# Moving the matmul operands of a two-layer hybrid-attention kernel to other byte places in SBUF

## The chip, the cores and the metric

The kernel runs on one core of a Trainium2 chip. The metric is the device time of one execution in microseconds (us). Before the change three runs took 823.54, 824.45 and 826.3 us; the median is 824.45 us.

## What is computed

Two transformer layers on 256 tokens of width 1024, all in float32. Each layer modulates its input by six vectors made from `silu(c) @ w_ada`, projects it, runs a top-k sparse attention and a latent attention, merges them by gates, and ends in a convolutional feed-forward block. Both halves close with a layer norm over a residual. Cut to what matters here:

```python
for l in range(DEPTH):                                   # DEPTH = 2
    mod = jax.nn.silu(c) @ w_ada[l] + b_ada[l]
    sh1, sc1, g1, sh2, sc2, g2 = jnp.split(mod[:, None, :], 6, axis=-1)
    h = x * (1.0 + sc1) + sh1
    y = token_mixer(h, ...)                              # h @ w_in, dsa and mla attention, gates, w_out
    x = layer_norm(DEEPNORM_ALPHA * x + g1 * y, ln1_g[l], ln1_b[l])
    h = x * (1.0 + sc2) + sh2
    y = conv_ffn(h, w_up[l], conv_w[l], conv_b[l], w_down[l])
    x = layer_norm(DEEPNORM_ALPHA * x + g2 * y, ln2_g[l], ln2_b[l])
```

## The kernel before

All weights lie in one stream in HBM. `load` (line 206) fetches them in pieces of up to 1 MB into four `raw` buffers through SyncE's queue. TensorE is to multiply in one pass per product, on four-byte operands of reduced precision (`float32r`), so each weight piece of 1024 columns is split: ScalarE copies its rounded part into a tile `hi` (line 241), VectorE subtracts that from the raw piece into a tile `lo` (line 242). There are four buffers of each. The activations are split in the same way into pairs: `hh` and `hl` for the input of a projection (lines 422 and 423), `nh` and `nl` for the normed inputs of the latent attention, `ybh`/`ybl` and `yah`/`yal` for the attention outputs, and six pairs `h2h`/`h2l` for the hidden layer of the feed-forward block.

`mm3` (line 284) is the heart of the kernel: three matmuls per product, `hi` by `hh`, `hi` by `hl` and `lo` by `hh`. The weight half, 128 columns of 4 bytes in each partition, is the operand that is loaded into the array; the activation half, 256 columns, is streamed through it. In the profile every such matmul is one LDWEIGHTS (row PEld) and one MATMUL (row PE), both of line 286. The load for a matmul goes on while the matmul ahead of it is streaming. In the value projection (line 606) the roles are exchanged: `hh`/`hl` are loaded and `hi`/`lo` are streamed. In line 592, 512 columns of `hi`/`lo` are streamed against `nh`/`nl`. Logits, transposes, sums and three pieces of `w_ada` (line 258) are plain float32 matmuls.

The order within a layer: `g1` (first projections), `qa` and `va` with the scoring, `uq`/`uk`/`uv` with the top-k search, the gates `ga`/`gb` woven with the two attentions, the branches `wb`/`wa`, `wo` with the layer norm, `up` and eighteen `upp` groups of 48 matmuls, `dn` with the second layer norm. A scheduler sets the order of the instructions on each engine, and gives each tile its place.

Places are given out pool by pool: first the pool `cp` of lasting tiles, then `wp` of streamed weights and scratch, then `ap_` of activations. In a pool each tag has its buffers in the order in which tags were first used, each rounded up to 32 bytes; every partition has the same places. The lines in question:

```python
cp = ctx.enter_context(tc.tile_pool(name="cp", bufs=1))                                  # 141
wp = ctx.enter_context(tc.tile_pool(name="wp", bufs=1))                                  # 142
ap_ = ctx.enter_context(tc.tile_pool(name="ap", bufs=1))                                 # 143
...
t = wp.tile([P, 2048], F32, name=f"raw{u}", tag="raw", bufs=RAW)                         # 206
...
hi = wp.tile([P, 1024], F32R, name=f"hi{i}", tag="whi", bufs=NHI)                        # 235
lo = wp.tile([P, 1024], F32R, name=f"lo{i}", tag="wlo", bufs=NLO)                        # 236
...
for p in passes:                                                                         # 285
    PE.matmul(out, whl[p // 2][:, wcol], xhl[p % 2][xsl], start=start and p == 0, stop=stop and p == 2,
              skip_group_check=True)
...
hh[0] = ap_.tile([P, KD, T], F32R, name=f"hh{name}", tag="hh")                           # 422
hh[1] = ap_.tile([P, KD, T], F32R, name=f"hl{name}", tag="hl")                           # 423
...
iw8 = ap_.tile([P, 2, HEADS], F32, name=new("iw8"), tag="iw8")                           # 484
```

Slices of a weight half start at multiples of 512 bytes in its tile, slices of an activation half at multiples of 1024 bytes, so modulo 256 bytes every slice has the place of its tile.

Of the kernel before, what the change touches and what calls it, by code (L numbers as in the profile page):

```python
# [9 lines left out]
F32 = mybir.dt.float32  # L10
# [7 lines left out]
P = 128  # L18
# [4 lines left out]
HEADS = 8  # L23
# [116 lines left out]
def _build(nc, tc, ctx, stream, xt, cbc, ctr, posl, vecs, cst, outp, dbg=None):  # L140
    cp = ctx.enter_context(tc.tile_pool(name="cp", bufs=1))
    wp = ctx.enter_context(tc.tile_pool(name="wp", bufs=1))
    ap_ = ctx.enter_context(tc.tile_pool(name="ap", bufs=1))
# [5 lines left out]

    def bank(tag, name):  # L150
        return pp.tile([P, 512], F32, name=name, tag=tag, bufs={"mm": 3, "at": 4, "st": 1}[tag])


    pos_i = wp.tile([P, 64 + T], I32, name="pos_i", tag="cv", bufs=4)
# [93 lines left out]
    def gap_fill(which, after):  # L248

        if which not in GAPS:  # L250
            return
        l, j = GAPS[which]
        advance(first[("adap", l, j)] + 1)
        b = bank("at", f"adap{l}{j}")
        raw = raws[uidx[("adap", l, j)]]
        with tc.issue_after(after.ins):
            for k in range(KD):
                PE.matmul(b[:, :T], ct[:, k:k + 1].to_broadcast([P, P]), raw[:, k * T:(k + 1) * T],  # L258
                          start=(k == 0), stop=(k == KD - 1))
        sc = wp.tile([P, P], F32, name=f"adapx{l}{j}", tag="mt", bufs=1)  # L260
        for n in range(2):
            V.scalar_tensor_tensor(out=sc, in0=b[:, n * P:(n + 1) * P], scalar=1.0, in1=ident, op0=OP.mult, op1=OP.mult,
                                   accum_out=mod[l][:, j + n:j + n + 1])
        V.tensor_add(mod[l][:, j:j + 2], mod[l][:, j:j + 2], vcol(l, V_BADA + j, 2))
# [25 lines left out]
    for h in range(2):  # L290
        b = bank("at", f"cb{h}")
        PE.matmul(b, onerow, crow[:, h * 512:(h + 1) * 512], start=True, stop=True)
        S.activation(cb[:, h * 512:(h + 1) * 512], b, AF.Silu)
# [82 lines left out]
    def bias_block(n):  # L376
        sb, half, q = ((0, 0, 0), (0, 0, 1), (0, 1, 0), (0, 1, 1), (1, 0, 1), (1, 1, 1))[n]
        b = bank("st", f"bb{n}")
        for gl in range(16):
            g = sb * 32 + half * 16 + gl  # L380
            st = steps[g // 8][:, g % 8, q * P:(q + 1) * P] if g < 32 else steps[4 + (g - 32) // 16][:, g % 16]
            for j in range(3):
                PE.matmul(b[:, gl * 32:gl * 32 + 32], st, dparts[j], start=(gl == 0 and j == 0), stop=(j == 2),
                          skip_group_check=True)
        o = (0 if q == 0 else P) + sb * P + half * 64
        S.activation(biast[:, :, o:o + 64].rearrange("p h s -> p s h"), b.rearrange("p (s h) -> p s h", h=HEADS), AF.Copy)
# [55 lines left out]
    def layer(l, hchunk, xres):  # L442
        new = lambda s: f"{s}{l}"
# [37 lines left out]

        qa = big("qa", new("qa"))
        va = ap_.tile([P, 2, 512], F32, name=new("va"), tag="va")
        iw8 = ap_.tile([P, 2, HEADS], F32, name=new("iw8"), tag="iw8")
        scr = ap_.tile([P, 384], F32, name=new("scr"), tag="scr")
        selm = ap_.tile([P, 384], BF, name=new("selm"), tag="selm")
        nhl = (big("g0", new("nh"), F32R), big("g1", new("nl"), F32R))
# [346 lines left out]
        for i in range(UPAIRS):  # L834
            if i >= X0:
                lnst["x"](i - X0)
            run(kinner(("upp", l, i), 2, 4, 2, hx2, lambda j, b, i=i: queue.append((G2 // 2 + i, b)),
                       tag="at" if i % 7 < 3 or i % 7 == 6 else "mm", name=new(f"upp{i}")))
# [187 lines left out]
    for l in range(L):  # L1026
        nxt, st = layer(l, nxt, x)
        x = st and st["x"]
# [118 lines left out]
```

## Time and profile before

| | |
|---|---|
| median of three runs | 824.45 us |
| the profiled execution | 823.38 us |
| its span, first to last instruction | 821.6 us |
| TensorE matmul busy (PE) | 797.2 us, 97% |
| TensorE weight load busy (PEld) | 769.2 us, 94% |
| VectorE busy | 684.5 us, 83% |
| ScalarE busy | 514.1 us, 63% |
| DMA, share of 16 engines | 62.5%, 222 GB/s |

The profile is that of one execution. Matmuls are pipelined: the duration of one (280 ns) is longer than the time from the start of one to the start of the next, and it is the latter, the slot, that counts. It is read from a stretch of n matmuls as the time from the first start to the last, divided by n-1, or from a piece of the chain of waits, which merges n matmuls that follow each other without a gap, as its time divided by n.

### The profile page before, as it was taken

To read this page: it belongs to the slowest core of one execution; us is meant where nothing else is said; L and a number is where in the kernel's file an instruction comes from. 1 tells how busy PE (TensorE), PEld (TensorE's weight loads), DVE (VectorE), ACT (ScalarE), POOL (GpSimd) and SP (SyncE) were. 2 spreads that over 40 slices of the span, in tenths; PEclk is the share of its full clock that TensorE was granted. 3 is DMA by queue.
4 is the path that set the end of the run, shared out by engine and by line. 5 is a ranking of instruction groups with operands and counts; after the bars stand their busy time and mean duration, and the time that the engine had idled before them with its cause. 6 is when DMAs were issued, how large, how long until landed. Compare 5 with 4: busy or idle time off the path is not lost.

```text
span 821.6 us, 16736 instructions
## 1 busy us (share of the span) xinstructions
PE 797.2 (97%) x6708; PEld 769.2 (94%) x6708; DVE 684.5 (83%) x1377; ACT 514.1 (63%) x898; POOL 0.2 (0%) x4
## 2 busy tenths in 40 slices
PE   5999999999999999999999999999999999999996
PEld 3898899999999999999999898998999999999995
DVE  6878798989988998888888897756988798897664
ACT  5987566565578676653547757656457876675452
POOL 0000000000000000000000000000000000000000
PEclk9999999999999999999999999999999999999998
DMA  8885758877745565578778756745555555565621
GB/s 299 303 331 199 231 185 297 295 273 285 252 164 201 189 227 200 175 276 292 280 264 293 234 189 211 295 162 202 209 168 192 184 182 200 195 211 186 211 72 51
DMA packets 29727, 182.07 MB, mean 222 GB/s; under 512 B 3857, under 2 KB 5841, under 8 KB 10578
## 3 DMA queue, kind: packets, MB, share of 16 engines
q1 hardware_dynamic: 29650, 181.01, 62.5%
q8 instruction: 52, 0.85, 0.4%
q14 instruction: 25, 0.20, 0.1%
HBM read 178.84 MB, written 1.05 MB: 219 GB/s over the span
## 4 chain that ended last, share of the span: by engine, by line
PE 82%; DVE 10%; ACT 4%; issue 2%; DMA 2%; SPq 0%; ACTq 0%; DVEq 0%
PE dn L286 15%; PE up L286 5%; PE g L286 5%; DVE lo L242 3%; DMA raw<-stream 2%; ACT hi L241 1%; PE wo L286 1%; DVE raw L227 1%; PE adap L258 1%; ACT step L374 1%; PE bl L652 1%; PE qa11b L286 1%; PE wo01b L286 1%; PE qa00b L286 1%; PE gb21b L286 1%
## 5 line engine op out<-in xcount | busy, mean ns | idle before, releaser
L241 ACT ACTIVATE hi<-raw 128x1024 fp32r<-128x1024 f32 (+3 forms) x255 | 254.9, 1004 | 206.0 <-PE dn L286 41.3
L242 DVE TENSOR_TENSOR lo<-raw,hi 128x1024 fp32r<-128x1024 f32 (+3 forms) x255 | 293.4, 1156 | 77.1 <-ACT hi L241 75.8
L227 DVE SCALAR_TENSOR_TENSOR raw<-raw,cb 128x1024 f32<-128x1024 f32 x90 | 107.6, 1219 | 15.5 <-DMA raw<-stream 10.3
L286 PE MATMUL dn<-h2l,hi 128*128 128x256 f32 x352 | 98.7, 280 | 0.0
L286 PE MATMUL dn<-h2h,lo 128*128 128x256 f32 x352 | 98.6, 280 | 0.0
L286 PE MATMUL dn<-h2h,hi 128*128 128x256 f32 x352 | 98.5, 280 | 0.0
L286 PEld LDWEIGHTS dn<-h2l,hi 128*128 128x128 f32 x352 | 66.2, 188 | 0.0
L286 PEld LDWEIGHTS dn<-h2h,lo 128*128 128x128 f32 x352 | 66.1, 188 | 0.1
L286 PEld LDWEIGHTS dn<-h2h,hi 128*128 128x128 f32 x352 | 66.2, 188 | 0.0
L286 PE MATMUL g<-hhm,hi 128*128 128x256 f32 x168 | 46.1, 293 | 5.5 <-ACT hhm L1016 5.4
L286 PE MATMUL g<-hhm,lo 128*128 128x256 f32 x168 | 44.8, 287 | 0.0
L286 PE MATMUL g<-hlm,hi 128*128 128x256 f32 x168 | 42.9, 282 | 0.0
L286 PEld LDWEIGHTS g<-hhm,hi 128*128 128x128 f32 x168 | 32.0, 195 | 7.7 <-ACT hhm L1016 7.2
L671 ACT ACTIVATE pr<-pr,mx 128x128 f32<-128x128 f32 x64 | 28.4, 447 | 12.0 <-DVE mx L668 11.9
L286 PE MATMUL up<-hhf,lo 128*128 128x256 f32 x128 | 34.9, 279 | 0.0
L286 PE MATMUL up<-hhf,hi 128*128 128x256 f32 x128 | 34.7, 281 | 0.0
L286 PE MATMUL up<-hlf,hi 128*128 128x256 f32 x128 | 33.3, 280 | 0.0
L286 PEld LDWEIGHTS g<-hhm,lo 128*128 128x128 f32 x168 | 31.8, 196 | 0.0
L286 PEld LDWEIGHTS g<-hlm,hi 128*128 128x128 f32 x168 | 30.3, 188 | 0.1
L286 PEld LDWEIGHTS up<-hhf,hi 128*128 128x128 f32 x128 | 23.8, 188 | 0.5 <-DVE hhf L969 0.5
L286 PEld LDWEIGHTS up<-hhf,lo 128*128 128x128 f32 x128 | 24.1, 188 | 0.0
L374 ACT ACTIVATE step<-posf,thr 128x256 bf16<-128x256 f32 (+1 forms) x64 | 23.2, 443 | 1.4 <-DVE thr L342 1.4
(904 smaller groups left out, 2667.8 us busy)
## 6 DMA issues: line engine op xcount, KB each, us to landing
raw<-stream SPq DMA_DIRECT2D x149, 1024.0 KB, 5.0
raw<-stream SPq DMA_DIRECT2D x21, 768.0 KB, 4.5
raw<-stream SPq DMA_DIRECT2D x5, 512.0 KB, 4.1
raw<-stream SPq DMA_DIRECT2D x4, 384.0 KB, 3.5
kT<-rl SPq DMA_DIRECT2D x8, 128.0 KB, 4.5
XB<-xt SPq DMA_DIRECT2D x3, 256.0 KB, 7.2
out<-XA SPq DMA_DIRECT2D x3, 256.0 KB, 2.5
XB<-xt SPq DMA_DIRECT2D x2, 128.0 KB, 6.7
```

The lines of the kernel that those rows point to most:

```text
L227: V.scalar_tensor_tensor(out=raw[:, c:c + D], in0=raw[:, c:c + D], scalar=1.0, in1=cb, op0=OP.mult, op1=OP.mult, accum_out=mod[l][:, j:j + 1])
L241: S.activation(hi[:, a:e], raw[:, c + a:c + e], AF.Copy)
L242: x = V.tensor_sub(lo[:, a:e], raw[:, c + a:c + e], hi[:, a:e].bitcast(F32))
L258: PE.matmul(b[:, :T], ct[:, k:k + 1].to_broadcast([P, P]), raw[:, k * T:(k + 1) * T], start=(k == 0), stop=(k == KD - 1))
L286: PE.matmul(out, whl[p // 2][:, wcol], xhl[p % 2][xsl], start=start and p == 0, stop=stop and p == 2, skip_group_check=True)
L374: S.activation(st, posf[:, 64 + (0 if g < 32 else P):], AF.Sign, bias=thr[:, g:g + 1])
L652: PE.matmul(bs[e][:, P:384], q[:, P:T], k, start=False, stop=True, skip_group_check=True)
L671: S.activation(p[:, sl], p[:, sl], AF.Exp, bias=mx[:, j:j + 1], scale=-1.0, accum_out=ssum[:, h, j:j + 1])
```

## The change

Two tiles are added that no instruction reads or writes: 24 floats (96 bytes) as the first tile of `wp`, and 232 floats (928 bytes) as the first of `ap_`. And `iw8`, of which 64 bytes are used, is made 256 bytes long. No instruction, wait, shape or engine is changed: the rows of each engine in the two built programs are the same one for one, apart from the line numbers, which are 4 higher behind line 153.

```diff
+    wp.tile([P, 24], F32, name="wpad", tag="wpad", bufs=1)
+    ap_.tile([P, 232], F32, name="apad", tag="apad")
+
+
     pos_i = wp.tile([P, 64 + T], I32, name="pos_i", tag="cv", bufs=4)
...
         va = ap_.tile([P, 2, 512], F32, name=new("va"), tag="va")
-        iw8 = ap_.tile([P, 2, HEADS], F32, name=new("iw8"), tag="iw8")
+        iw8 = ap_.tile([P, 8, HEADS], F32, name=new("iw8"), tag="iw8")
         scr = ap_.tile([P, 384], F32, name=new("scr"), tag="scr")
```

What the two built programs give as places, as the first byte within a partition modulo 256:

| tiles | before | after |
|---|---|---|
| `hi`, `lo`, `raw`, scratch of tags cv, pr, rl, rsA | 160 | 0 |
| scratch of tag sq | 192 | 32 |
| `hh`, `hl`, `ybh`, `ybl`, `yah`, `yal`, `qa`, `ka`, `va`, `vb`, `iq`, `misc`, `qT`, `kT`, pairs 0 to 4 of `h2h`/`h2l` | 192 | 192 |
| `nh`, `nl`, pair 5 of `h2h`/`h2l`, gates, `scr`, `selm`, squares and sums of the layer norms | 0 | 192 |
| `XA`, `XB`, `cb` (pool `cp`) | 0 | 0 |
| `ones1k`, `future`, `biast`, `rope` (pool `cp`) | 160 | 160 |

## Rows read from the trace of the kernel before

**Rows 1.** The page: span, busy time of each engine, slices of TensorE and its clock
```profile
span 821.6 us, 16736 instructions
...
PE 797.2 (97%) x6708; PEld 769.2 (94%) x6708; DVE 684.5 (83%) x1377; ACT 514.1 (63%) x898; POOL 0.2 (0%) x4
...
PE   5999999999999999999999999999999999999996
...
PEclk9999999999999999999999999999999999999998
```

**Rows 2.** The page: the chain that ended last, by engine
```profile
PE 82%; DVE 10%; ACT 4%; issue 2%; DMA 2%; SPq 0%; ACTq 0%; DVEq 0%
```

**Rows 3.** Chain from 268 to 300 us: start, length, what, merged count
```profile
270.87 5.60 PE upp30b L286 x48
276.47 5.60 PE upp40b L286 x48
282.07 5.60 PE upp50b L286 x48
```

**Rows 4.** Timeline of TensorE: start, length; first and last of twenty matmuls
```profile
99.35 0.28 PE L286 MATMUL uq<-nh,hi 128*128 128x256 f32 x1
...
101.63 0.29 PE L286 MATMUL uk<-nl,hi 128*128 128x256 f32 x1
```

**Rows 5.** Timeline of TensorE: first and last of forty matmuls of line 606
```profile
89.95 0.28 PE L606 MATMUL va<-hi,hlm 128*128 128x256 f32 x1
...
94.57 0.28 PE L606 MATMUL va<-hi,hlm 128*128 128x256 f32 x1
```

**Rows 6.** Timeline of TensorE: streams of 512 columns; first and end of five slots
```profile
105.36 0.40 PE L592 MATMUL uv<-lo,nh 128*128 128x512 f32 x1
...
106.52 0.28 PE L286 MATMUL ga00b<-hhm,hi 128*128 128x256 f32 x1
```

**Rows 7.** Chain, plain float32: six transposes of 128 columns; sixteen matmuls of 256
```profile
526.31 0.66 PE bt L680 x6
```
```profile
228.03 3.45 PE adap L258 x16
```

**Rows 8.** Windows over the span, of line 286 and then of line 606 alone
```profile
0.00:821.60 821.60, 667.08 (x5520) 653.79 (x5520) 1.00 0.63 222
```
```profile
0.00:821.60 821.60, 24.35 (x192) 23.18 (x192) 1.00 0.63 222
```

**Rows 9.** Groups of VectorE by form: equal work on tiles at different places
```profile
L962 DVE TENSOR_TENSOR XB<-XB,rsA 128x256 f32<-128x256 f32 x21 | 8.4, 420 | 0.0
...
L972 DVE TENSOR_TENSOR hlf<-rl,hhf 128x256 fp32r<-128x256 f32 x16 | 6.4, 421 | 0.7 <-ACT rl L971 0.7
...
L755 DVE TENSOR_TENSOR gate<-gate,gate 128x512 f32<-128x512 f32 x8 | 5.2, 687 | 0.0
L760 DVE TENSOR_TENSOR hlg<-gate,hhg 128x512 fp32r<-128x512 f32 x8 | 5.2, 687 | 0.0
```

**Rows 10.** Windows by stage: length, busy PE, PEld, DVE, ACT, POOL, clock, DMA share, GB/s
```profile
107.00:180.00 73.00, 72.83 (x615) 69.31 (x613) 65.77 (x185) 45.41 (x109) 0.00 (x0) 1.00 0.77 283
180.00:228.00 48.00, 47.90 (x397) 47.29 (x397) 45.84 (x65) 24.75 (x30) 0.00 (x0) 1.00 0.68 241
228.00:354.00 126.00, 126.00 (x1067) 125.38 (x1066) 112.48 (x208) 89.60 (x151) 0.00 (x0) 1.00 0.56 194
354.00:424.00 70.00, 69.11 (x563) 67.60 (x562) 61.41 (x103) 31.65 (x42) 0.00 (x0) 1.00 0.83 297
```

## The prediction

> **What bounds the kernel now.** I read the page from the top. TensorE's matmul row is busy for 797.2 of 821.6 us, nearly every slice of it shows a 9, and the granted clock is a 9 in all slices but the last, so TensorE runs at the upper of its two levels, 2.4 GHz [rows 1]. The chain that ended last says the same from the other side: 82% of the span is PE, 10% VectorE, 4% ScalarE, 2% DMA [rows 2]. So the time is made of TensorE slots that follow each other, and a change that touches no instruction can only act through the length of a slot, or through the length of work on the other engines.
>
> The slot is the figure to look at next. In the `upp` groups 48 matmuls take 5.60 us without a gap: 116.7 ns each [rows 3]. Here `hhf`/`hlf` at place 192 are streamed and `hi`/`lo` at place 160 are loaded. The same shape stands in the trace with other places. In `uq` and `uk` the streamed `nh`/`nl` lie at 0, the loaded halves at 160: 19 slots in 2.28 us, 120.0 ns each [rows 4]. In line 606 the roles are exchanged, 160 is streamed and 192 loaded: 39 slots in 4.62 us, 118.5 ns each [rows 5]. All three are 128 by 128 by 256 columns, all run without a gap; what differs is the operands, and with them the places. That is the trace's evidence that a place in SBUF costs something, and it is a difference of 3.3 ns in 116.7, near 3%.
>
> How far could a slot fall? Plain float32 gives a hold. Six transposes of 128 columns take 0.66 us, 110.0 ns each; sixteen matmuls of 256 columns take 3.45 us, 215.6 ns each [rows 7]. The second 128 columns cost 105.6 ns, two clocks of 2.4 GHz per column, and 4.4 ns are left as the fixed part. Operands that stream one column per clock would need 256 / 2.4 = 106.7 ns and those 4.4 ns: 111.1 ns. Nothing in the trace goes below that. A second hold is line 592, which streams 512 columns against one loaded half: five slots in 1.16 us, 232 ns each [rows 6]. Against line 606, which streams from the same place, the further 256 columns cost 232 - 118.5 = 113.5 ns, and in that time no load of 128 columns has to go on beside them.
>
> **The change part by part.**
>
> *The weight halves go from 160 to 0 under a stream at 192.* Line 286 holds 5520 such matmuls, line 606 another 192 [rows 8]. The new pair, 192 streamed and 0 loaded, stands nowhere in the trace, so I bound it: 111.1 ns from below, 120.0 ns from above. The value that I take is 113.5 ns, the price of 256 columns with no load beside them. I choose it because the new pair differs from the three known ones in one thing: in each of those an operand lies at 160, which is no multiple of 64, so that a half of 512 bytes starts and ends within such a piece, and reaches into three pieces of 256 bytes. At 0 it fills two of them exactly. This is an argument from the addresses, not a measurement, and the chances below treat it so. The slot then falls by 116.7 - 113.5 = 3.2 ns.
>
> How many slots count? PE is 82% of the chain, 673.7 us, of 797.2 us that it is busy: 84.5%. Of 5520 matmuls that makes 4664, so each ns of slot is worth 4.66 us. The term is 3.2 x 4.66 = 14.9 us.
>
> *`nh`, `nl` and pair 5 of `h2h`/`h2l` go from 0 to 192.* They join the others. There are 96 matmuls of `uq`, 24 of `uk` and, with two of the 22 chunks of `dn` and 1056 matmuls, 96 there: 216. They stood at 120.0 instead of 116.7 ns, so they gain 3.3 ns more: 216 x 0.845 x 3.3 = 0.6 us.
>
> *Line 606: streamed place from 160 to 0, loaded stays at 192.* Again an unseen pair; between 111.1 and 120.0 ns against 118.5 now, that is from -1.2 to +0.2 us on 162 counted slots. I take nothing.
>
> *The other engines.* `raw`, `hi`, `lo` and the scratch tags move for ScalarE and VectorE too, `sq`, gates, `scr` and `selm` as well. VectorE shows no sign of minding: 256 columns take 420 ns from 0 and 160 into 0, and 421 ns from 160 and 192 into 192; 512 columns take 687 ns from gates at 0 and 687 ns from a gate at 0 and a tile at 192 into 192 [rows 9]. I cost this at nothing, with 1 ns in 420 as its bound: 0.24% of 684.5 us of VectorE, 1.6 us were all of it on the path, of which VectorE has a tenth. Transfers are the same in number and size, and go to other addresses in the same buffers.
>
> *What is late next.* A faster TensorE needs the halves sooner. From 180 to 228 us VectorE is busy for 45.84 of 48 us, from 107 to 180 for 65.77 of 73, from 354 to 424 for 61.41 of 70, with the DMA engines at 0.83 there [rows 10]. The first of these can shrink by 4% at most before `lo` is late, less with waits between its instructions. From 228 to 354 VectorE has 13.5 us to spare. I take a fifth of the gain as lost to this: 15.5 x 0.2 = 3.1 us.
>
> **The sum** is 14.9 + 0.6 - 3.1 = 12.4 us. Against the profiled execution, 823.38 us (a span of 821.6 and 1.8 around it), that is 811.0 us. The median of three runs stands 1.1 us above that execution, so I predict 812.0 us for the median. With the slot at 111.1 it would be 5.6 x 4.66 x 0.8 = 20.9 us and the small term, 803 us.
>
> **The rivals.**
>
> *The places meet worse: slower.* Take the place streamed minus the place loaded, modulo 256. It is 32 for the 116.7 ns, 96 for the 120.0, and 224 for the 118.5 [rows 3 to 5]. After the change it is 192. If that distance is what counts, the new pair lies next to 224, on the far side from 32, and the present place is already the best of the three that the trace shows. The slot is then 118.5 to 120.0 ns, up by 1.8 to 3.3: 8.4 to 15.4 us, with no cover, since TensorE is what all wait for. That gives 833 to 840 us, 836 in the middle. It decides as soon as the new slot is over 116.7. Against it: three points are few, the operands differ in more than places, and none of the three has both operands on multiples of 64.
>
> *Nothing that counts: the same.* The further 256 columns of line 592 still cost 113.5 ns and not 106.7, so most of what a slot has over 106.7 may belong to the streaming itself, wherever the load reads [rows 6]. Then the slot stays at 116.7, only the 216 gain, and the median is 823.8 us. The Trainium skill, "SBUF — State Buffer", section "Who interferes with whom", would have it so: TensorE has two read ports of its own, one for the streamed operand and one for LDWEIGHTS, and never waits on another reader. By that page the sum is zero and the time 824.5 us. The trace does not agree as it stands: 116.7, 118.5 and 120.0 ns for one shape [rows 3 to 5].
>
> *VectorE takes over.* The slot falls as forecast, but `lo` is late in all stages at nine tenths, and two thirds of the gain turn into waits of PE for line 242. Left are 15.5 / 3 = 5.2 us: 819 us. For it speaks VectorE's 95% from 180 to 228 us; against it that the 126 us of `up`, and most of the second layer, have room [rows 10].
>
> **How the numbers follow.** About 0.3%, 2.5 us, is what a measurement of this kernel can tell from no change. I give the forecast 0.4, VectorE taking over 0.1, the same slot 0.2, the worse meeting 0.3. The first two are faster by more than the bound: 0.5. The third is within it: 0.2. The fourth is slower: 0.3. Cases of both signs hold most of the chance, so the forecast's own range stands apart: 803 (slot 111.1) to 819 us. The range for the whole runs from 801, a little under the lower bound, to 838 us, in the upper half of the slower case; about one in ten lies beyond each end.
>
> **What would show it.** The chain's `upp` pieces are the test: x48 in about 5.45 us if right, 5.60 if nothing happens, 5.69 or more if the places meet worse. `uq` and `uk` should read as `upp` does, since both now stream from 192 against 0; if they still differ, it is not the place that set them apart. MATMUL counts and the durations of lines 241 and 242 should stay as they are. VectorE's share of the chain should rise from 10% to 11 or 12%; well over that is VectorE taking over. I am wrong if the `upp` slot is at or above 116.7 ns, or if it falls while the span does not.

## The result and the profile after

The changed kernel took 816.18 us (median; 814.9 to 819.06) against 824.1 us for the four runs of the kernel before that were taken with it. The ratio is 0.9909, with a 95% interval of 0.9883 to 0.9934: faster by 0.7 to 1.2%. Measured once more later, in ten runs, the ratio was 0.9937 [0.9907, 0.9966]. Ratios here and below are of fast runs alone, while medians count every run, among them one slow run in each of two kernels below. The forecast was 812.0 us in a range of 801 to 838: sign and range hold, the gain came out smaller, some 8 us instead of 12.4. The profiled execution is one of 814.9 us.

The page of the changed kernel, its lines on the span, the busy time, TensorE's clock, the chain, and the groups that make `hi` and `lo`:

```profile
span 813.1 us, 16736 instructions
...
PE 787.8 (97%) x6708; PEld 759.6 (93%) x6708; DVE 683.3 (84%) x1377; ACT 514.1 (63%) x898; POOL 0.2 (0%) x4
...
PEclk9999999999999999999999999999999999999999
...
PE 73%; DVE 14%; DMA 5%; ACT 5%; issue 2%; SPq 0%; ACTq 0%; DVEq 0%
...
L245 ACT ACTIVATE hi<-raw 128x1024 fp32r<-128x1024 f32 (+3 forms) x255 | 254.8, 1004 | 194.8 <-PE dn L290 48.1
L246 DVE TENSOR_TENSOR lo<-raw,hi 128x1024 fp32r<-128x1024 f32 (+3 forms) x255 | 293.1, 1154 | 73.8 <-ACT hi L245 72.6
```

The same counts of instructions, the same clock, VectorE and ScalarE as busy as before within 1.2 us [rows 1]. What fell is PE, by 797.2 - 787.8 = 9.4 us, and the span by 8.5. So nearly all that TensorE saved reached the end. Line numbers are 4 higher: 290 is `mm3`, 610 the value projection.

The windows over the whole span for line 290 and for line 610 alone put the saving in its place:

```profile
0.00:813.10 813.10, 658.03 (x5520) 644.43 (x5520) 1.00 0.63 224
...
0.00:813.10 813.10, 24.05 (x192) 22.88 (x192) 1.00 0.63 224
```

Against [rows 8] line 290 fell by 667.08 - 658.03 = 9.05 us and line 610 by 0.3 us. Now the slot. The chain of the changed kernel, pieces in layer 0 and then in layer 1 (start, length, what, merged count):

```profile
111.50 5.65 PE ga10b L290 x48
...
275.61 5.65 PE upp40b L290 x48
...
379.94 37.58 PE dn L290 x319
...
507.72 5.44 PE ga21b L290 x48
...
664.21 5.44 PE upp41b L290 x48
...
764.91 36.16 PE dn L290 x319
```

This is what the forecast had not thought of. The same matmuls, on tiles at the same places, have **two slots**: 5.65 / 48 = 117.7 ns in `ga`, `upp` and `dn` of layer 0, and 5.44 / 48 = 113.3 ns in layer 1 (`dn`: 37.58 / 319 = 117.8 and 36.16 / 319 = 113.4). One is longer than the 116.7 ns of before [rows 3], the other is the 113.5 that was forecast. Most of the gain is therefore made in layer 1: `upp40b` begins 0.9 us earlier than before (275.61 against 276.47 in [rows 3]), and the chain of the kernel before has for the same group of layer 1

```profile
668.30 5.60 PE upp41b L286 x48
```

so that `upp41b` begins 4.1 us earlier, and the end comes 8.5 us earlier.

The timeline of TensorE in the changed kernel, `uq` and `uk` first, the first and last of 25 matmuls, then line 610, the first and last of 36 in layer 0 and of 37 in layer 1:

```profile
97.98 0.28 PE L290 MATMUL uq<-nh,lo 128*128 128x256 f32 x1
...
100.81 0.28 PE L290 MATMUL uk<-nh,lo 128*128 128x256 f32 x1
...
76.78 0.28 PE L610 MATMUL va<-hi,hhm 128*128 128x256 f32 x1
...
80.75 0.28 PE L610 MATMUL va<-hi,hlm 128*128 128x256 f32 x1
...
479.79 0.28 PE L610 MATMUL va<-hi,hlm 128*128 128x256 f32 x1
...
484.02 0.28 PE L610 MATMUL va<-hi,hlm 128*128 128x256 f32 x1
```

`uq` and `uk` take 2.83 / 24 = 117.9 ns where they took 120.0 [rows 4], as `upp` of the same layer does. Line 610, which took 118.5 ns [rows 5], has two slots as well: 3.97 / 35 = 113.4 ns in layer 0 and 4.23 / 36 = 117.5 ns in layer 1 (117.8 from the trace's starts in whole nanoseconds).

### The profile page after: what moved, and what is told of

Its sections match the earlier page's. It is cut to its first block, busy times and chain, and to the rows that moved or that the text cites. A ratio compares the mean times of both kernels' runs of the same rounds, so it can differ in the third digit from the quotient of the medians.

```text
span 813.1 us, 16736 instructions
## 1 busy us (share of the span) xinstructions
PE 787.8 (97%) x6708; PEld 759.6 (93%) x6708; DVE 683.3 (84%) x1377; ACT 514.1 (63%) x898; POOL 0.2 (0%) x4
## 4 chain that ended last, share of the span: by engine, by line
PE 73%; DVE 14%; DMA 5%; ACT 5%; issue 2%; SPq 0%; ACTq 0%; DVEq 0%
PE dn L290 15%; PE up L290 6%; DVE lo L246 5%; DMA raw<-stream 5%; DVE raw L231 2%; ACT hi L245 2%; PE wo L290 1%; PE g L290 1%; ACT step L378 1%; DMA pr<-misc 1%; PE adap L262 1%; PE bl L656 1%; PE gb11b L290 1%; PE gb10b L290 1%; PE qa00b L290 1%
## 5 line engine op out<-in xcount | busy, mean ns | idle before, releaser
L245 ACT ACTIVATE hi<-raw 128x1024 fp32r<-128x1024 f32 (+3 forms) x255 | 254.8, 1004 | 194.8 <-PE dn L290 48.1
L246 DVE TENSOR_TENSOR lo<-raw,hi 128x1024 fp32r<-128x1024 f32 (+3 forms) x255 | 293.1, 1154 | 73.8 <-ACT hi L245 72.6
L231 DVE SCALAR_TENSOR_TENSOR raw<-raw,cb 128x1024 f32<-128x1024 f32 x90 | 107.5, 1219 | 12.4 <-DMA raw<-stream 7.1
```

The costliest lines, as they stand in the source:

```text
L231: V.scalar_tensor_tensor(out=raw[:, c:c + D], in0=raw[:, c:c + D], scalar=1.0, in1=cb, op0=OP.mult, op1=OP.mult, accum_out=mod[l][:, j:j + 1])
L245: S.activation(hi[:, a:e], raw[:, c + a:c + e], AF.Copy)
L246: x = V.tensor_sub(lo[:, a:e], raw[:, c + a:c + e], hi[:, a:e].bitcast(F32))
```

## The experiments

All are compared with the kernel before on the same chip. "Distance" is the place streamed minus the place loaded, modulo 256 bytes. It was 32 before (192 against 160), and 96 where `nh`, `nl` and pair 5 at 0 were streamed; after the change it is 192. In the value projection, where the roles are exchanged, it was 224 before and is 64 after.

### Which part of the change it is

**The two pads alone.** `iw8` keeps its 64 bytes, so `nh`, `nl` and pair 5 of `h2h`/`h2l` stay at 0 (distance 0 now); all else is as in the change.

```diff
+    wp.tile([P, 24], F32, name="wpad", tag="wpad", bufs=1)
+    ap_.tile([P, 232], F32, name="apad", tag="apad")
```

> The two pads without the longer iw8: hi and lo at 0, hh and hl at 192, nh, nl and pair 5 of h2h/h2l still at 0. In the trace of the changed kernel a stream of line 286 holds one of two slots from its start to its end, 113.3 ns or 117.8 ns; in the trace before it was 116.7 or 117.8 ns. If the place of the halves under the stream makes the gain, long streams (upp, wa, dn) show 113.3 or 117.8 here too and the time is 814 to 820 us, with uq and chunk 5 of dn at a slot of their own, since 0 is streamed over 0. If the tiles behind iw8 made the gain, the slots are 116.7 and the time is 823 to 826 us.

Measured: 818.0 us (4 runs, 810.63 to 818.83), ratio 0.9897 [0.9849, 0.9946]. The chain has 5.44 us for 48 `upp` matmuls in both layers:

```profile
273.78 5.44 PE upp30b L288 x48
...
665.82 5.44 PE upp41b L288 x48
```

The whole gain is there without `iw8`. In `uq`, where 0 is now streamed over 0, 45 of the 48 neighbouring pairs without a gap in layer 0 stand 120 ns apart.

**The longer `iw8` alone.** Halves stay at 160, everything that is streamed against them lies at 192 (distance 32).

```diff
-        iw8 = ap_.tile([P, 2, HEADS], F32, name=new("iw8"), tag="iw8")
+        iw8 = ap_.tile([P, 8, HEADS], F32, name=new("iw8"), tag="iw8")
```

> The longer iw8 without the pads: all streamed tiles at 192, hi and lo at 160 as before. If the place of the halves under the stream makes the gain: upp stays at 116.7 ns, uq and chunk 5 of dn come from 120.0 to 116.7, and the time is 822 to 824 us. If the tiles behind iw8 (gates, scr, selm, pair 5) made the gain: 815 to 818 us.

Measured: 824.1 us (10 runs), ratio 0.9993 [0.9971, 1.0015]; nothing that can be measured. Its chain, `upp` in layer 0 and `dn` in layer 1:

```profile
270.86 5.60 PE upp30b L286 x48
...
764.92 42.82 PE dn L286 x367
```

`upp` is unchanged, but `dn` takes 42.82 / 367 = 116.7 ns a slot. In the kernel before the same stage reads

```profile
764.97 44.59 PE dn L286 x378
```

that is 44.59 / 378 = 118.0 ns, more than the 96 matmuls of pair 5 at 120.0 among 1056 explain. So the few slots of pair 5 had lengthened their neighbours too: in `dn` of layer 0 before, 94 slots ahead of a piece of pair 5 have a mean of 116.7 ns, and 114 behind it one of 117.8. This is the first sign that a slot depends on what went ahead of it. Nor is 116.7 the only slot at distance 32 where no other distance is near: with the longer `iw8` alone, 126 slots of `wo` in layer 1 without a gap have a mean of 117.8.

**The halves alone.** The pad for the weight halves stands directly ahead of `hi`, so that `raw` and the scratch of tags cv, pr and rl stay at 160.

```diff
+    ap_.tile([P, 232], F32, name="apad", tag="apad")
...
+            if not split:
+                wp.tile([P, 24], F32, name="wpad", tag="wpad", bufs=1)
             hi = wp.tile([P, 1024], F32R, name=f"hi{i}", tag="whi", bufs=NHI)
...
-        iw8 = ap_.tile([P, 2, HEADS], F32, name=new("iw8"), tag="iw8")
+        iw8 = ap_.tile([P, 8, HEADS], F32, name=new("iw8"), tag="iw8")
```

> The 96 bytes stand between the scratch and the halves, so that hi and lo go to 0 and raw, cv, pr and rl stay at 160; iw8 long, streams at 192. If the places matter to TensorE alone: the slots 113.3 and 117.8 ns and the time of the changed kernel, 814 to 820 us. If the gain came from VectorE, ScalarE or the transfers into raw: 822 to 825 us, with 116.7 ns in upp.

Measured: 818.49 us (7 runs), ratio 0.991 [0.9875, 0.9945], the gain of the whole change. So it is TensorE's operands that count; `raw` and the scratch left at 160 add nothing that can be seen, and the tiles that move with `iw8` gave nothing by themselves. Its chain, `ga` and `upp` of layer 0, then `ga` and `upp` of layer 1:

```profile
116.43 5.44 PE ga10b L289 x48
...
275.03 5.65 PE upp30b L289 x48
...
507.36 5.65 PE ga11b L289 x48
...
664.43 5.44 PE upp31b L289 x48
```

TensorE's operands have the places of the change, but now `ga` has the short slot in layer 0 and the long one in layer 1, the reverse of the changed kernel.

### Multiples of 64, or the distance

Two kernels keep the distance of 192 with no operand on a multiple of 64: halves at 32 and streams at 224; halves at 160 and streams at 96.

```diff
# halves at 32, streams at 224
+    wp.tile([P, 32], F32, name="wpad", tag="wpad", bufs=1)
+    ap_.tile([P, 232], F32, name="apad", tag="apad")
# halves at 160, streams at 96
+    ap_.tile([P, 232], F32, name="apad", tag="apad")
# both
+        iw8 = ap_.tile([P, 8, HEADS], F32, name=new("iw8"), tag="iw8")
```

> Everything 32 bytes further: hi and lo at 32, streams at 224, so the distance streamed minus loaded is 192 as in the changed kernel, but no operand lies on a multiple of 64. If the distance decides: slots of 113.3 or 117.8 ns, 814 to 820 us. If it takes both operands on multiples of 64, as the prediction argued: 116.7 ns or more, 823 us or more.

> hi and lo stay at 160, all streams go from 192 to 96: again the distance 192, reached from the other side and with neither at a multiple of 64. If the distance alone decides: slots of 113.3 or 117.8 ns in the long streams of line 286 and 810 to 822 us. If the place of the loaded half decides by itself: 116.7 ns and 823 to 826 us.

Measured: 815.99 us (4 runs, 810.02 to 823.52), ratio 0.9877 [0.9803, 0.9951], and 815.55 us (4 runs, 812.02 to 819.28), ratio 0.9892 [0.9843, 0.994]. `upp` has 5.44 us in both layers of both; the chain of the second:

```profile
268.51 5.44 PE upp30b L287 x48
...
665.09 5.44 PE upp51b L287 x48
```

113.3 ns at places of which none is a multiple of 64. That reason of the forecast is refuted.

The other distances keep the streams at 192 and move the halves, with `wpad` and `apad` together 1024 bytes and `iw8` as in the change: `wpad` of 8 floats puts the halves at 192, of 56 at 128, of 40 at 64, of 32 at 32, of 16 at 224.

```diff
+    wp.tile([P, 8], F32, name="wpad", tag="wpad", bufs=1)
+    ap_.tile([P, 248], F32, name="apad", tag="apad")
```

> hi and lo at 192 under streams at 192, distance 0, both on multiples of 64. Where 0 is streamed over 0 in the run with the pads alone, the slots are 120 ns. If the distance decides: about 120.0 ns in all of line 286, 836 to 842 us. If the prediction's argument on multiples of 64 holds: 113.3 or 117.8 ns as in the changed kernel, 810 to 822 us.

> hi and lo at 128 under streams at 192, distance 64, both on multiples of 64. Line 606 of the changed kernel has this distance and shows 116.5 ns in the mean, with single slots of 113 and 118. If the distance decides, line 286 shows the same two here and the time is 810 to 824 us; if the roles of the operands matter too, another slot.

> hi and lo at 64 under streams at 192, distance 128, both on multiples of 64. No run has shown this distance. If only distances 0 and 96 are bad (120 ns), it lies between 113.3 and 117.8 ns, 810 to 826 us; if what counts repeats every 128 bytes, it is as distance 0: 120 ns, 836 to 842 us.

> The halves at 32, all streams at 192: distance streamed minus loaded 160, the only multiple of 32 but 224 that line 286 has not shown. Theory (the distance sets which slots are possible): a value of its own, the same for every dense stream or one of two; the time is 823.4 + 4.66 us per ns from 116.7 to the slot found: 113.3 everywhere gives 808, 117.8 everywhere 829, 120.0 everywhere 839. Rival (a half at a multiple of 64 bytes is what gains): 32 is none, so no gain, 824 us or more.

> The halves at 224, all streams at 192: distance 224 in line 286, 32 in line 606. Theory (distance, whichever line and tile): line 286 has the slot that line 606 had before at distance 224, 118.5 ns, and line 606 has 116.7, the slot that line 286 had before at 32: about 832 us. Rival (the slot belongs to the line, that is to the roles and the order of its operands): line 286 stays at 116.7 and line 606 at 118.5, 824 us.

The chains of the five, one `upp` group each, in the order of the expectations:

```profile
274.05 5.76 PE upp30b L288 x48
```
```profile
274.49 5.65 PE upp30b L288 x48
```
```profile
277.32 5.69 PE upp30b L288 x48
```
```profile
273.00 5.70 PE upp30b L288 x48
```
```profile
272.36 5.68 PE upp30b L288 x48
```

| halves, streams | distance | `upp` slot, ns | runs | median, us | ratio to before |
|---|---|---|---|---|---|
| 192, 192 | 0 | 120.0 | 2 | 838.09 | 1.0149 [1.0091, 1.0208] |
| 160, 192 (before) | 32 | 116.7 | 3 | 824.45 | |
| 128, 192 | 64 | 117.7 | 8 | 827.63 | 1.0035 [1.001, 1.0059] |
| 64, 192 | 128 | 118.7 | 2 | 834.85 | 1.011 [1.0055, 1.0166] |
| 32, 192 | 160 | 118.7 | 10 | 829.37 | 1.0049 [1.0029, 1.007] |
| 0, 192 (the change) | 192 | 113.3 or 117.7 | 4 | 816.18 | 0.9909 [0.9883, 0.9934] |
| 224, 192 | 224 | 118.3 | 10 | 830.37 | 1.0077 [1.0053, 1.0101] |

Halves at 192 and at 64, on multiples of 64 as their streams are, make the kernel slower; the best distance is reached from 0, 32 and 160 alike. Two of the five expectations missed. Distance 128 lies in neither of its two ranges: 118.7 ns, longer than 117.8, and 834.85 us. Distance 64 has the two slots that were expected, but its time is 3.6 us above the range, since all its long streams took the longer one. The shorter stands in `uq` of layer 0, first and last of 48:

```profile
98.32 0.28 PE L288 MATMUL uq<-nh,hi 128*128 128x256 f32 x1
...
103.65 0.28 PE L288 MATMUL uq<-nh,lo 128*128 128x256 f32 x1
```

5.33 / 47 = 113.4 ns. Two slots are thus no mark of distance 192, and an `upp` group shows only one of them: with halves at 32, the last 383 slots of `dn` in layer 1 without a gap have a mean of 117.3 ns where `upp` has 118.7.

Line 608 of two of these kernels, the value projection with its roles exchanged, shows that it is the distance and not the line. The timeline of the kernel with halves at 224, first and last of 33 matmuls; there the distance in this line is 32:

```profile
485.31 0.28 PE L608 MATMUL va<-hi,hhm 128*128 128x256 f32 x1
...
489.04 0.28 PE L608 MATMUL va<-hi,hlm 128*128 128x256 f32 x1
```

and with halves at 128, first and last of 37, distance 192:

```profile
485.25 0.28 PE L608 MATMUL va<-hi,hlm 128*128 128x256 f32 x1
...
489.33 0.28 PE L608 MATMUL va<-hi,hlm 128*128 128x256 f32 x1
```

3.73 / 32 = 116.6 ns and 4.08 / 36 = 113.3 ns. With halves at 224 the two lines have exchanged slots in layer 1: `upp` has 118.3 where the value projection had 118.5 [rows 5], and the value projection 116.6 where `upp` had 116.7 [rows 3]. In layer 0 of that kernel line 608 stands at 117.8, the other slot of distance 32. With halves at 128 the value projection has the short slot, while `upp` beside it has 117.7. Two more distances agree with line 286 when the roles are exchanged: 82 slots of line 608 in layer 1 have a mean of 119.9 ns at distance 96 (halves at 32) and of 118.6 at 128 (halves at 64).

### Which of the two slots a stream gets

**The changed kernel once more**, nothing edited.

> The changed kernel itself, profiled once more. Theory (a gapless stream falls at its start into a slot of 113.3 or of 117.8 ns, and which one is not settled by places and order alone): the long streams are again at 113.3 or 117.8 and at nothing else, but not the same ones; of ga00 to ga20, up and dn of layer 0, which stood at 117.8, at least one is at 113.3, or one of layer 1 at 117.8; the runs scatter over 810 to 822 us. Rival (the program settles it, by the instructions ahead of each stream): the same streams in the same slots, runs within 0.3% of each other near 815.

Measured: 819.49 us (10 runs, 814.07 to 824.31), ratio 0.9937 [0.9907, 0.9966]; the profiled run is of 814.61 us. Its chain, `ga`, `upp` and `dn` of layer 0, `ga` and `upp` of layer 1:

```profile
111.76 5.44 PE ga10b L290 x48
...
270.07 5.65 PE upp30b L290 x48
...
379.92 36.16 PE dn L290 x319
...
507.53 5.44 PE ga21b L290 x48
...
663.93 5.44 PE upp41b L290 x48
```

Only 5.65 and 5.44 again, but `ga` and `dn` of layer 0 have gone from 117.7 to 113.3 ns. The same program gives the same stream either slot. Two of the ten runs, 823.51 and 824.31 us, lie above the 822 that was expected. The rival, that the program settles it, falls; and with it any hope of reading this kernel's gain to a tenth of a per cent from a few runs.

**A few slots of another distance, to throw the stream out of its slot.** The timeline of the kernel with the two pads alone, `dn` of layer 0, ahead of and behind a piece of pair 5, twelve matmuls at distance 0 (the first two rows stand 15 slots apart, the last two nine):

```profile
384.88 0.28 PE L288 MATMUL dn<-h2h,lo 128*128 128x256 f32 x1
...
386.65 0.28 PE L288 MATMUL dn<-h2h,lo 128*128 128x256 f32 x1
...
387.96 0.28 PE L288 MATMUL dn<-h2l,hi 128*128 128x256 f32 x1
...
388.98 0.28 PE L288 MATMUL dn<-h2l,hi 128*128 128x256 f32 x1
```

1.77 / 15 = 118.0 ns ahead of it, 1.02 / 9 = 113.3 behind it; `dn` of layer 1 does the same. Without such a piece no stream does. In the five profiles with every stream of line 286 at 192 (the change twice, the halves alone, and the two kernels on no multiple of 64), the starts in the traces give 216 stretches of twenty or more slots in which none reaches 120 ns. From their ninth slot on, 139 stay in the short slot and 77 in the long one; none changes. The last kernel puts such a piece into `up`: twelve matmuls of the first `upp` group stream copies of two input chunks that lie at 0. It is the kernel of the two pads with this added:

```diff
+            if k == 4:
+                kn = (big("g0", new("knh"), F32R), big("g1", new("knl"), F32R))
+                for j in range(2):
+                    S.activation(kn[j][:, 0:2], hx2[j][:, 0:2].bitcast(F32), AF.Copy)
...
-    def kinner(key, parts, kper, nt, xhl, evict, tag="mm", name=""):
+    def kinner(key, parts, kper, nt, xhl, evict, tag="mm", name="", first=None):
...
-                    mm3(banks[n // 2][:, (n % 2) * T:(n % 2 + 1) * T], whl, xhl,
+                    mm3(banks[n // 2][:, (n % 2) * T:(n % 2 + 1) * T], whl, first if first and k < 2 else xhl,
...
-                       tag="at" if i % 7 < 3 or i % 7 == 6 else "mm", name=new(f"upp{i}")))
+                       tag="at" if i % 7 < 3 or i % 7 == 6 else "mm", name=new(f"upp{i}"),
+                       first=kn if i == 0 else None))
```

> The kernel of pads_only (halves at 0, streams at 192, pair 5 at 0) with twelve matmuls of the first upp group of each layer streaming copies of two input chunks that lie at 0, that is at distance 0, 120 ns a slot; four copies on ScalarE are added, some 3 us in all, beside other work. Theory (a few slots of another distance throw a stream out of its slot, and from distance 0 it comes back into 113.3, as dn did after both of its pair 5 pieces in pads_only): behind the twelve, upp and what follows stand at 113.3 in both layers, whatever they stood at before; up and dn can no longer be slow together, the runs lie closer than the 810 to 822 us of the same places without it, near 811 to 814 where the granted clock is 0.997 or more. Rival (the slot is drawn anew at each disturbance): behind the twelve at least one of the two layers may stand at 117.8, and the runs scatter as before, 810 to 822. Second rival (the copies or the twelve cost more than they give): 818 us or more.

Measured: 813.75 us (6 runs, 811.54 to 818.67), ratio 0.9864 [0.984, 0.9888]. The timeline of TensorE in layer 0, around the twelve:

```profile
259.22 0.28 PE L288 MATMUL up<-hhf,hi 128*128 128x256 f32 x1
...
259.93 0.28 PE L288 MATMUL upp00b<-knh,hi 128*128 128x256 f32 x1
...
261.37 0.29 PE L288 MATMUL upp00b<-hhf,hi 128*128 128x256 f32 x1
261.49 0.28 PE L288 MATMUL upp00b<-hlf,hi 128*128 128x256 f32 x1
261.61 0.28 PE L288 MATMUL upp00b<-hhf,lo 128*128 128x256 f32 x1
...
262.29 0.28 PE L288 MATMUL upp00b<-hhf,lo 128*128 128x256 f32 x1
```

Six slots ahead of the twelve take 0.71 us, 118 ns each; the twelve 1.44 us, 120.0 each; two more 120 each; from 261.61 on six slots take 0.68 us, 113 each. The stream that had begun in the long slot goes on in the short one, and the `upp` groups behind it have it in layer 0 as in layer 1:

```profile
265.63 5.44 PE upp10b L288 x48
...
667.30 5.44 PE upp41b L288 x48
```

In layer 1 `up` stood in the short slot already, and the twelve left it there. In the two kernels with pieces at distance 0, ten such pieces are followed by eighteen or more slots without a gap; four streams came to them in the long slot and six in the short, and all ten went on in the short one. The effect ends with the stream: `dn` of layer 1 began again in the long slot behind a gap, which the expectation had not allowed, until its own piece of pair 5 brought it back. The copies cost ScalarE 517.8 - 514.1 = 3.7 us, beside other work. The four of its six runs that had a mean granted clock of 0.997 or more lie between 811.5 and 814.0 us; the five such runs of the changed kernel, when it was measured again, between 814.1 and 823.5. The profiled run is the longest of the six, 818.67 us, at a granted clock of 0.989. This is the lowest median here. Its interval lies below that of the repeated measurement of the change; it overlaps those of the first measurement, of the two pads alone and of the two kernels on no multiple of 64, so what is shown of the twelve is their effect on the slots, not a gain in time over those kernels.

## Why the prediction was right, and where it was not

**The bound.** Right: TensorE's slots made the time, and each ns was priced well. With 4.66 us per ns on 823.4 us, slots of 120.0, 117.7 and 118.3 ns in all of line 286 give 839, 828 and 831 us; the kernels that had them took 838.09, 827.63 and 830.37. Of the two with 118.7 ns in `upp`, which gives 833, halves at 64 took 834.85, in two runs at a granted clock of 0.992, and halves at 32, where some streams stood at 117.3, took 829.37.

**Term 1, the slot of the moved halves.** This is the term that was mis-sized, and the reason for it fell. It took one slot for all, 113.5 ns, a fall of 3.2. The forecast's own test, `upp` groups of about 5.45 us and wrong at or above 116.7 ns a slot, came out both ways: 5.44 in layer 1, 5.65 in layer 0. Over the 5148 neighbouring pairs of such matmuls without a gap in the trace of before, and 5348 after, the mean start-to-start time fell from 116.87 to 115.15 ns, by 1.72: 4664 x 1.72 = 8.0 us instead of 14.9. The short slot was met to 0.2 ns, but only part of the streams had it; the mean between 113.3 and 117.7 puts it at (117.7 - 115.15) / 4.4 = 58%. The reason given, both operands on multiples of 64, predicts gains for halves at 192 and 64 and none at 32 under 224 or 160 under 96, and the runs show the opposite. To meet 113.3 was therefore luck: the 113.5 was the difference of two rows that lie at different distances (160 in line 592, 224 in line 606), and no run ties it to the load. The sign hangs on the streams as well: with the long slot throughout, the price above gives 828 us, as halves at 128 took, though none of the fourteen runs of the change came that high.

The reading of 116.7 ns as the slot also hid something. It is a mean: of the 864 neighbouring pairs in the `upp` groups of layer 0 before, 216 stand 113 or 114 ns apart and 216 stand 120 apart, in an order that repeats every four, while in `wa` all are 116 or 117. So starts 113 ns apart stood in the trace already.

**Term 2, the 216 matmuls.** Right in kind: `uq` and `uk` left 120.0 and read as `upp` of their layer does. They stood at 119.7 ns (mean of 205 gapless pairs), 2.8 above the others. Since Term 1 counts their common fall, what they add is 216 x 0.845 x 2.8 = 0.5 us, against 0.6.

**Line 606.** Costed at nothing, gained 0.3 us.

**The other engines.** Nothing, as forecast. Lines 245 and 246 take a mean of 1004 and 1154 ns in the profile after, 1004 and 1156 before; the kernel with `raw` and most of the scratch left in place has the whole gain.

**The loss to waits.** A fifth was taken, 3.1 us. The terms add up to 8.0 + 0.5 + 0.3 = 8.8 us and the span fell by 8.5: 0.3 us, which one execution of each kernel cannot tell from nothing. VectorE's share of the chain rose from 10 to 14%, more than the 11 to 12 expected, and DMA's from 2 to 5 [rows 2]; but the chain's shares grew more than the time did.

**The rivals.** *The places meet worse* had the right quantity, the distance, and read the wrong value for 192 from its neighbour 224. Its prices hold where they could be tried: halves at 224 took 830.37 us with `upp` at 118.3 ns. Distance 192 does not lie on a slope between its neighbours, 118.7 at 160 and 118.3 at 224. *Nothing that counts* fell with the seven slots of one shape. By the rule of the Trainium skill that stood beside it ("SBUF — State Buffer", "Who interferes with whom": TensorE's two read ports are independent, and it waits on no one) all of these kernels would take the same time; the traces here do not agree, 113.3 to 120.0 ns and 813.75 to 838.09 us. *VectorE takes over* did not happen.

**What stays open.** Why a distance gives the slot that it gives, and why 32, 64, 160 and 192 give two. What at the start of a stream sets which of them it gets was not found: the same program gave both. Why halves at 128 put all long streams into the long slot, in a kernel whose eight runs lie within 826.09 to 830.81 us, is open too. Distance 96 was not run as the place of all streams; [rows 4] and the value projection with halves at 32 show it. Whether twelve matmuls are needed, or fewer do, was not tried.

## What to carry to other kernels

Where one engine's equal instructions follow each other without a gap, compare their start-to-start time at different places of the operands before trusting one figure; here the distance between the streamed and the loaded tile, modulo 256 bytes, was worth 3% of a slot either way, and about 1% of the kernel's time, with no instruction changed. A lone tile at another distance can set the pace of its neighbours, so look behind odd pieces as well as at them. A time that scatters from run to run may be one program with two stable paces: split the trace into its streams before explaining the mean.

## What was not expected of the hardware

- A gapless stream of these matmuls at distance 192 runs at 113.3 or at 117.7 ns and keeps its slot to its end where no piece at another distance lies in it (216 of 216 stretches in five profiles), `dn` of layer 0 for 319 matmuls at 117.8 in one execution and at 113.4 in another of the same program.
- The slot by distance has no order: 120.0 at 0, 116.7 or 117.8 at 32, 113.4 or 117.8 at 64, 120.0 at 96 [rows 4], 118.7 at 128, 118.7 or 117.3 at 160, 113.3 or 117.7 at 192, 118.3 at 224; it is the same with exchanged roles at 32, 64, 96, 128, 192 and 224.
- A slot read over many matmuls can be the mean of a repeating order: 116.7 in `upp` before is made of starts 113 to 120 ns apart.
- Twelve matmuls at distance 0 took a stream at distance 192 from 117.7 to 113.3 ns in each of the four cases here: `up` of layer 0 and `dn` of layer 1 in the last kernel, and `dn` of both layers in the kernel with the two pads alone.
